# A transformer layer in split fp32: squares by tokens, roots and column sums off GpSimd, stored weight sums, and attention's transposes ahead of its scores

## The chip, the cores and the metric

One core of a Trainium2 chip runs the whole layer. The metric is the device time of one execution in microseconds, the median of three runs. Engines: TensorE (PE in the rows) multiplies, VectorE (DVE) and ScalarE (ACT) compute on tiles, GpSimd (POOL) does element-wise work and issues some DMAs, SyncE (SP) issues the other DMAs. SBUF is the on-chip memory, PSUM the memory that TensorE writes to, in banks of 128 x 512 fp32.

## The reference

A layer over 2048 tokens of width 1024, all in fp32: chunked attention with 16 heads of 64 and a learned relative bias, then a SwiGLU feed-forward part of width 2816.

```python
def rms_norm(x, g):
    y = xf * lax.rsqrt(jnp.mean(xf * xf, axis=-1, keepdims=True) + RMS_EPS)
    return (y * g.astype(jnp.float32)).astype(x.dtype)

h = rms_norm(x, g_pre_mix[i])
m = chunk_relpos_attention(h, w_qkv[i], w_o[i], rel_bias[i // N_MIXERS])
x = x + rms_norm(m, g_post_mix[i])
h = rms_norm(x, g_pre_ffn[i])
x = x + rms_norm(swiglu(h, w_gate[i], w_up[i], w_down[i]), g_post_ffn[i])
```

A chunk of 64 tokens attends to its own and the eight chunks before it, so a block of 128 queries sees 640 keys, five blocks of 128.

## The kernel before

**Products.** Each fp32 operand is split into a high and a low half (`split`, `split_part`; `hi` by ScalarE, `lo` by VectorE), and each product is three matmuls of 128x512 (`products`, L184 to L186). The large products run in seven instead of eight block products (Strassen's scheme): the blocks of activations and weights are B11, B21, T1, T2, B22, T4, T3, where T and S stand for sums of blocks. The weights' sums S1 to S4 are made by GpSimd in `block_items` (L816), in place in the raw tiles that were loaded; the splits then read them.

**Projection** (`project`). The 2048 tokens are two groups g of two 512-token blocks n. For each group `values_of` makes the values and `queries_keys` the queries and keys. The norm's gain goes into the activations; its root, one number per token, is applied behind the product: by `emit_v` for the values (tokens on partitions) and by `emit_qk` for q and k (tokens along the row, so a multiplication with `rows_of[n]`, the root spread over all partitions by four transposes, `spread`, tile prs, L336). The root of block n comes from squares of the activations on their way through `prep` (ScalarE's `sq`, L251), added up by GpSimd (`total`, L252), summed over partitions by TensorE (pssq, L269) and raised to -1/2 by GpSimd (L276). Group 1's activations are prepared while group 0's q and k are made. In `closing` VectorE takes a PSUM bank into `terms` (L1201), and `emit_qk` multiplies (L418), splits (L420, L421) and stores.

**Attention** (`Attend`). 32 jobs (four quarters n of 512 queries, eight pairs of heads p), four slots t each, one for each block of 128 queries. `scores` writes both heads' 640 scores to one tile `st` of three PSUM banks; VectorE adds the bias and finds the row's extreme (L506, `nmax`), ScalarE takes the exponentials (L510), VectorE the reciprocals (L514), GpSimd scales (L517). `transposed` transposes key blocks 0 to 3 of each head into `tt` (two banks, L532), copied out by VectorE for head 0 (L535) and by ScalarE for head 1 (L537), and then the fifth block of both heads into the free end of the scores' bank (L543, copied by ScalarE, L544). `output` multiplies with the values (L559). Between these stands filler, `fill`: the output projection of the quarter before, cut into small pieces. The first quarter has no filler, and, as nothing precedes it, no fifth block.

**Feed-forward** (`gate_up`, `down`, two token groups; stream `back` brings the weights of each of 11 column units, once for each group).

**Order.** TensorE's order is the order in which the code is written. The other engines' order comes from a list scheduler over the same program, so a change in the code can reorder them. Background steps (`later`, `timed`, `roots`) are released by the amount of TensorE work done. `Stream.ahead` loads and splits weights some blocks ahead of their use; SP issues nearly all DMAs in one queue in order. Raw weight tiles come from a ring of 8 (`w4`) in the projection, of 6 in the feed-forward part.

Of the kernel before, what the change touches and what calls it, by code (L numbers as in the profile page):

```python
# [9 lines left out]
F32 = mybir.dt.float32  # L10
# [3 lines left out]
ALU = mybir.AluOpType  # L14
# [35 lines left out]
def trunk(  # L50
    ctx: ExitStack,
    tc: tile.TileContext,
    x: bass.AP,
    gains: bass.AP,
# [359 lines left out]
    def emit_qk(n, p, which, src, eng=dve):  # L414

        scale = (0.125, 1.0)[which]
        t = narrow("t")
        eng.tensor_tensor(t, src, rows_of[n], op=ALU.mult)  # L418
# [10 lines left out]

    def scores_bank():  # L430

        if "S" not in phase:
            phase["S"] = phase["psa"].tile([P, 3 * HALF], F32, name="st", bufs=1)
        return phase["S"]

    class Attend:
# [45 lines left out]
        def scores(self, ib):  # L482
# [16 lines left out]
            rows = ap.tile([P, 4], F32, tag="rows", name="rows", bufs=3)  # L499
# [21 lines left out]
        def transposed(self, ib, fill):  # L521
# [16 lines left out]
            fill()  # L538
            if self.prev:
                r, b = blocks[4]  # L540
                tt = scores_bank()[:, 1280:1536].rearrange("p (h q) -> p h q", h=2)
                for h in range(2):
                    pe.transpose(tt[:, h, :], sc[h][:, b * P : b * P + P], ident)  # L543
                act.activation(self.pT[:, :, 4, cols], tt, AF.Copy)  # L544
# [42 lines left out]
    class Blocks:  # L587
# [58 lines left out]
        def build(self, part, w, prep):  # L646
# [32 lines left out]
            def t2(k):  # L679
# [5 lines left out]
                pool.tensor_tensor(b, b, c, op=ALU.subtract)  # L685
                pool.tensor_tensor(a, d, a, op=ALU.subtract)
# [118 lines left out]

    def block_items(src, key, early=True, ahead=None):

        r = {}

# [5 lines left out]
        def sum_(to, a, b, op=ALU.add):  # L815
            last_pool[0] = pool.tensor_tensor(r[to], r[a], r[b], op=op)  # L816

        def make(n):
# [3 lines left out]
            if n == ("B11" if early else "B21"):  # L822
                sum_("A21", "A21", "A22")
                sum_("A11", "A11", "A21")
            if n == "B21":
                sum_("A12", "A12", "A11")
            if n == "T2":
                sum_("A21", "A11", "A22", ALU.subtract)
# [10 lines left out]
    def v_items(g):  # L839

        parts = [block_items(w_v[h], f"v{g}{h}", False, {n: (8, 2 + h) for n in BLOCKS}) for h in range(2)]
# [288 lines left out]
    def values_of(g, b, big):  # L1130
# [9 lines left out]
        def after(name, m, pt):  # L1140
# [31 lines left out]
    def queries_keys(g, b, big, after):  # L1172
# [13 lines left out]
        for c in range(NPAIR // 2):  # L1186
# [12 lines left out]
            def closing(pts, terms, n, p, op=ALU.subtract):  # L1199
                def go(i):  # L1200
                    dve.tensor_tensor(terms[i], pts[i], terms[i], op=op)  # L1201
                    emit_qk(n, p, i, terms[i], pool)
# [26 lines left out]
    def project():  # L1229
# [10 lines left out]
        def prepare(g):  # L1240
            def prep(t, k, x_):
                if k == 0:
                    totals[2 * g + t] = (
                        io("total") if g else phase["fp"].tile([P, HALF], F32, tag="tot", name="total", bufs=2)
                    )
                add_square(x_, totals[2 * g + t], k == 0, pool)
# [16 lines left out]

        front.ahead(-8)
# [8 lines left out]
        for k, (_, f) in enumerate(build(0, "B11")):  # L1273
            f()
            if k == 0:
                front.ahead(-2)
        later.extend(timed(
            (1.0, build(0, "B21", 2.5)), (14.0, build(0, "T1", 3.5)[:1]), (17.0, roots(0, 2.0)),
            (20.0, build(0, "T1", 3.0)[1:]), (30.0, build(0, "T2", 4.0)), (47.0, roots(1, 4.0)),
            (53.0, build(0, "B22", 2.0)), (62.0, build(0, "T4", 2.0)), (71.0, build(0, "T3", 1.0)),  # L1280
            (100.0, [(0.0, bias_rows)]),
        ))
        for g in range(NG):
            big = xp.tile([P, 10, HALF], F32, tag="big", name="terms", bufs=1)
            yield from values_of(g, groups[g], big)
            drain()

            def after(name, g=g):
# [288 lines left out]
```

## Time and profile before

| | |
|---|---|
| three runs | 2672.91, 2688.82, 2688.07 us; median 2688.07 |
| profiled execution | 2675.12 us on the device, span 2673.4 us, mean TensorE clock 0.964 |
| busy | TensorE 90%, VectorE 65%, ScalarE 43%, GpSimd 30% of the span |
| DMA | 461.06 MB moved, 172 GB/s in the mean |
| stages | projection 0 to 592 us, attention 592 to 1305, feed-forward to the end |

Rows of groups give: line, engine, operation, output and inputs by the program's names, count, then busy us and mean ns of one, then the engine's idle us just before them and what ended it. Rows of waits give the waiting engine and line, what it waited for, us in total, times and the longest. Rows of a timeline give start, duration, engine and line, and in brackets the idle time before and its releaser.

### The profile page before, as it was taken

The page shows a single profiled execution, that of the slowest core. Times are in us where ns is not written, and L with a number is a line of the kernel's source. Part 1 is how long each engine was busy: PE and PEld are TensorE (multiplying, and loading weights), DVE is VectorE, ACT ScalarE, POOL GpSimd, SP SyncE. Part 2 cuts the span into 40 slices and gives each one's busy share as a digit, 9 for nine tenths or more (in the row PEclk, how much of TensorE's full clock was granted, in tenths as well). Part 3 has the DMA queues.
Part 4 walks back from the last instruction along what each step waited for, and adds up shares of the span by engine and source line. Part 5 has one row for each costly group of instructions (what it writes and reads, how often), then busy time and mean ns, then how long its engine had stood idle before and what let it go on. Part 6 is the DMA issues. An engine that isn't in the chain of part 4 may idle for free. (4 is left out here: it accounts for less than half of the span.)

```text
span 2673.4 us, 33185 instructions
## 1 busy us (share of the span) xinstructions
PE 2419.3 (90%) x11466; PEld 1938.0 (72%) x11466; DVE 1739.1 (65%) x2470; ACT 1153.4 (43%) x2039; POOL 809.5 (30%) x598
## 2 busy tenths in 40 slices
PE   7988779977888788887899999999999999999998
PEld 5776658765566566666687778888887788888887
DVE  7755866655544454555598768767756778765567
ACT  6522543325554444445453233336543233333444
POOL 7434755543322332232143222210003222220002
PEclk7999889988999999999999999999999999999999
DMA  4344439969865675667345544327764354427554
GB/s 158 121 123 128 154 103 281 284 170 229 227 174 163 181 209 159 190 203 199 126 142 189 177 146 131 107 74 260 254 213 154 131 175 148 151 84 246 186 185 162
DMA packets 210921, 461.06 MB, mean 172 GB/s; under 512 B 24224, under 2 KB 40624, under 8 KB 206272
## 3 DMA queue, kind: packets, MB, share of 16 engines
q1 hardware_dynamic: 208640, 447.39, 53.5%
q0 software_dynamic: 2112, 11.54, 2.5%
q8 instruction: 91, 1.49, 0.2%
q14 instruction: 78, 0.64, 0.1%
HBM read 347.11 MB, written 134.79 MB: 180 GB/s over the span
## 5 line engine op out<-in xcount | busy, mean ns | idle before, releaser
L816 POOL TENSOR_TENSOR raw<-raw,raw 128x1024 f32<-128x1024 f32 x136 | 358.9, 2640 | 911.2 <-DMA raw<-in_w_gu 439.6
L517 POOL TENSOR_SCALAR sc<-sc,rows 128x640 f32<-128x640 f32 (+4 forms) x256 | 191.5, 762 | 465.0 <-DVE rows L514 297.0
L510 ACT ACTIVATE sc<-sc,nmax 128x640 f32<-128x640 f32 (+4 forms) x256 | 192.9, 754 | 218.4 <-DVE nmax L506 215.0
L506 DVE CUSTOM_DVE_ANT_0 sc<-st,bias 128x640 f32<-128x640 f32 (+2 forms) x248 | 175.9, 746 | 154.1 <-PE st L498 130.7
L497 PE MATMUL st<-k,q 128*128 128x512 f32 (+3 forms) x440 | 153.9, 362 | 113.5 <-ACT pT L544 95.3
L184 PE MATMUL pb<-hb,w_wg_T 128*128 128x512 f32 x528 | 207.3, 393 | 8.0 <-DVE terms L918 7.3
L186 PE MATMUL pb<-hb,w_wg_T 128*128 128x512 f32 x528 | 206.9, 392 | 0.0
L185 PE MATMUL pb<-hb,w_wg_T 128*128 128x512 f32 x528 | 206.6, 391 | 0.0
L497 PEld LDWEIGHTS st<-k,q 128*128 128x128 f32 x440 | 86.7, 197 | 146.0 <-ACT pT L544 117.3
L185 PE MATMUL pd<-a,w_d_T 128*128 128x512 f32 (+1 forms) x368 | 140.5, 382 | 1.8 <-DVE a L341 1.8
L186 PE MATMUL pd<-a,w_d_T 128*128 128x512 f32 (+1 forms) x368 | 140.6, 382 | 0.1
L920 ACT ACTIVATE terms<-terms 128x512 f32<-128x512 f32 x65 | 41.1, 632 | 230.7 <-DVE terms L918 230.7
L184 PE MATMUL pd<-a,w_d_T 128*128 128x512 f32 (+1 forms) x368 | 140.6, 382 | 0.0
L184 PE MATMUL pa<-hb,w_wg_B 128*128 128x512 f32 x352 | 137.3, 390 | 1.8 <-ACT terms L899 1.8
L186 PE MATMUL pa<-hb,w_wg_B 128*128 128x512 f32 x352 | 137.0, 389 | 0.0
L185 PE MATMUL pa<-hb,w_wg_B 128*128 128x512 f32 x352 | 136.9, 389 | 0.0
L532 PEld LDWEIGHTS tt<-ident,sc 128*128 128x128 f32 x928 | 110.2, 145 | 30.6 <-POOL sc L517 15.4
L498 PE MATMUL st<-k,q 128*128 128x512 f32 (+3 forms) x440 | 132.3, 333 | 0.0
L131 DVE TENSOR_TENSOR w_wg_T<-raw,w_wg_T 128x1024 fp32r<-128x1024 f32 x88 | 123.6, 1405 | 11.6 <-ACT w_wg_T L130 11.5
L559 PE MATMUL po<-pT,v 128*64 128x128 f32 (+3 forms) x864 | 130.6, 451 | 0.0
L532 PE MATMUL tt<-ident,sc 128*128 128x128 f32 x928 | 129.5, 282 | 0.0
L421 DVE SCALAR_TENSOR_TENSOR lo<-t,hi 128x512 fp32r<-128x512 f32 x64 | 72.8, 1137 | 76.8 <-ACT hi L420 76.7
(253 smaller groups left out, 6515.1 us busy)
## 6 DMA issues: line engine op xcount, KB each, us to landing
raw<-in_w_gu SPq DMA_DIRECT2D x88, 512.0 KB, 4.0
q<-q SPq DMA_DIRECT2D x62, 512.0 KB, 6.6
k<-k SPq DMA_DIRECT2D x55, 512.0 KB, 8.4
raw_a<-aT SPq DMA_DIRECT2D x88, 256.0 KB, 3.8
raw_d<-d_S SPq DMA_DIRECT2D x88, 256.0 KB, 3.5
bias<-ext_d SPq DMA_DIRECT2D x124, 144.0 KB, 8.8
aT<-T SPq DMA_DIRECT2D x66, 256.0 KB, 2.0
raw_d<-in_w_d SPq DMA_DIRECT2D x66, 256.0 KB, 4.0
```

What stands on the lines that cost most here:

```text
L131: dve.tensor_tensor(lo, raw, hi.bitcast(F32), op=ALU.subtract)
L184: pe.matmul(pt, a_hi, b_hi, start=first, stop=False, skip_group_check=go_on)
L185: pe.matmul(pt, a_hi, b_lo, start=False, stop=False, skip_group_check=go_on)
L186: pe.matmul(pt, a_lo, b_hi, start=False, stop=last, skip_group_check=go_on)
L497: pe.matmul(st[:, a:b], q[:, 2 * h, cols], kk[:, h, key], start=True, stop=False)
L498: pe.matmul(st[:, a:b], q[:, 2 * h + 1, cols], kk[:, h, key], start=False, stop=True)
L506: dve.tensor_tensor_reduce(out=sc[:, :n], in0=st[:, c0 : c0 + n], in1=rev, scale=-1.0, scalar=3.0e38, op0=ALU.add, op1=ALU.min, accum_out= ...
L510: act.activation(sc[:, :n], sc[:, :n], AF.Exp, bias=nmax, scale=-1.0, accum_out=rows[:, h : h + 1])
L517: last_pool[0] = pool.tensor_scalar(sc[:, :n], sc[:, :n], rows[:, 2 + h : 3 + h], 1.0, op0=ALU.mult, op1=ALU.mult)
L532: pe.transpose(tt[:, u, :], sc[h][:, b * P : b * P + P], ident)
L559: pe.matmul(po[heads[h], c0:c1], v[:, kb, c : c + 64], self.pT[:, h, r, c0:c1], start=m == 0, stop=m == len(terms) - 1,)
L816: last_pool[0] = pool.tensor_tensor(r[to], r[a], r[b], op=op)
```

## The change

Four things change.

1. The roots of blocks 1 to 3 are made from a second copy of the input, `xt`, with tokens on partitions: ScalarE squares a 128x1024 tile with its row sum as a by-product (`roots_by_tokens`), and GpSimd raises four columns to -1/2. Block 1 uses one spare tile for its four loads. Block 0 keeps the old way, with the adds on VectorE.
2. VectorE does what GpSimd did at three places: the multiplication by the root in `closing`, in place, the two subtractions of `t2`, and the addition of values in `after`.
3. Group 0 stores every weight sum to DRAM (`sums_d`) by a DMA that GpSimd issues; group 1 loads the stored sums (`stored_items`) and makes none, for the projection and for gate and up.
4. In attention a slot is now: transposes of slot t, scores of slot t + 3, filler, fifth block of slot t. Before: scores of slot t + 2, filler, transposes of slot t, filler, fifth block. The fifth block goes to a `tt` bank.

```diff
-    def emit_qk(n, p, which, src, eng=dve):
+    def emit_qk(n, p, which, src, t=None):
-        t = narrow("t")
-        eng.tensor_tensor(t, src, rows_of[n], op=ALU.mult)
+        if t is None:
+            t = narrow("t")
+        dve.tensor_tensor(t, src, rows_of[n], op=ALU.mult)
...
-                cuts = [(0, 512, 640), (640, 1024, 1280)]
+                cuts = [(P, 512, 768), (768, 1024, 1408)]
...
-            st = scores_bank()
+            st = phase["psa"].tile([P, 3 * HALF], F32, tag="S", name="st", bufs=1)
...
-                sc = ap.tile([P, 640], F32, tag="sc", name="sc", bufs=6)
-                nmax = ap.tile([P, 1], F32, tag="nmax", name="nmax", bufs=6)
+                sc = ap.tile([P, 640], F32, tag="sc", name="sc", bufs=8)
+                nmax = rows[:, 4 + h : 5 + h]
...
-            fill()
-            if self.prev:
-                r, b = blocks[4]
-                tt = scores_bank()[:, 1280:1536].rearrange("p (h q) -> p h q", h=2)
-                for h in range(2):
-                    pe.transpose(tt[:, h, :], sc[h][:, b * P : b * P + P], ident)
-                act.activation(self.pT[:, :, 4, cols], tt, AF.Copy)
+            self.rest = (sc, blocks[4], cols) if self.prev else None
+
+        def fifth(self):
...
+            tt = phase["psa"].tile([P, 4, P], F32, tag="tt", name="tt", bufs=2)
+            for h in range(2):
+                pe.transpose(tt[:, h, :], sc[h][:, b * P : b * P + P], ident)
+            act.activation(self.pT[:, :, 4, cols], tt[:, 0:2, :], AF.Copy)
...
-                pool.tensor_tensor(b, b, c, op=ALU.subtract)
-                pool.tensor_tensor(a, d, a, op=ALU.subtract)
+                dve.tensor_tensor(b, b, c, op=ALU.subtract)
+                dve.tensor_tensor(a, d, a, op=ALU.subtract)
...
+    def stored_items(src, key, ahead=None):
+        def load(n):
+            a = FACTOR[n]
+            t = phase["fp"].tile([P, 1024], F32, tag="w4", name="raw4", bufs=phase["w4"])
+            sp.dma_start(t, src[BLOCK_AT[a]] if a in BLOCK_AT else sums_d[key][a])
+            return t
...
-        def sum_(to, a, b, op=ALU.add):
-            last_pool[0] = pool.tensor_tensor(r[to], r[a], r[b], op=op)
+        def sum_(name, to, a, b, op=ALU.add):
+            pool.tensor_tensor(r[to], r[a], r[b], op=op)
+            last_pool[0] = pool.dma_start(sums_d[key][name], r[to])
...
-                pool.tensor_tensor(z[m], z[m], p1[m], op=ALU.add)
+                dve.tensor_tensor(z[m], z[m], p1[m], op=ALU.add)
...
-                    emit_qk(n, p, i, terms[i], pool)
+                    emit_qk(n, p, i, terms[i], terms[i])
...
-                add_square(x_, totals[2 * g + t], k == 0, pool)
+                if g == t == 0:
+                    add_square(x_, totals[0], k == 0)
...
+        def roots_by_tokens(n, w, back, room=None):
...
+            def load(b):
...
+                c[b] = room or phase["fp"].tile([P, D], F32, tag="w4", name="xt", bufs=phase["w4"])
+                sp.dma_start(c[b], xt[4 * n + b])
+
+            def use(b):
+                act.activation(c[b], c[b], AF.Square, accum_out=c["sum"][:, b : b + 1])
+
+            def root():
+                m = const.tile([P, 4], F32, tag="ms", name="ms", bufs=2)
+                dve.tensor_scalar(m, c["sum"], 1.0 / D, EPS, op0=ALU.mult, op1=ALU.add)
+                pool.tensor_tensor(rs[n], m, neg_half.to_broadcast([P, 4]), op=ALU.pow)
...
-            (20.0, build(0, "T1", 3.0)[1:]), (30.0, build(0, "T2", 4.0)), (47.0, roots(1, 4.0)),
-            (53.0, build(0, "B22", 2.0)), (62.0, build(0, "T4", 2.0)), (71.0, build(0, "T3", 1.0)),
+            (20.0, build(0, "T1", 3.0)[1:]), (30.0, build(0, "T2", 3.5)), (45.0, roots_by_tokens(1, 0.5, 2.0, spare)),
+            (52.0, build(0, "B22", 2.0)), (62.0, build(0, "T4", 2.0)), (71.0, build(0, "T3", 1.0)),
...
+            if g == 0:
+                later.extend(pause(50.0) + roots_by_tokens(2, 8.0, 4.0) + pause(10.0) + roots_by_tokens(3, 8.0, 4.0))
...
-                        (12.0, roots(2, 3.0)), (15.0, roots(3, 3.0)),
...
-        job.scores((t + 2) % 4)
...
-        fill(0.45 * share)
         if t > 0 and t % 4 == 0:
+            fill(0.45 * share)
             jobs[t // 4 - 1].output()
...
-        if t >= 0:
-            jobs[t // 4].transposed(t % 4, lambda: fill(0.55 * share))
-        if t < 0:
-            fill(0.55 * share)
+        job = jobs[t // 4]
+        job.transposed(t % 4)
+        ahead(t + AHEAD)
+        fill((0.55 if t % 4 == 0 else 1.0) * share)
+        job.fifth()
```

Three places show how instructions move. VectorE's order where group 0's q and k are closed, before (`terms` are the sums of q or k, `lo` the low half, `raw` and `w` a weight on its way to being split):

```order
84 L1201 TENSOR_TENSOR terms<-pb,terms 128x512
85 L421 SCALAR_TENSOR_TENSOR lo<-t,hi 128x512
86 L1201 TENSOR_TENSOR terms<-pb,terms 128x512
87 L131 TENSOR_TENSOR w_w_T_1178<-raw_1015,w_w_T_1178 128x1024
88 L421 SCALAR_TENSOR_TENSOR lo<-t,hi 128x512
```

The same place after the change:

```order
110 L1224 TENSOR_TENSOR terms<-pb,terms 128x512
111 L420 TENSOR_TENSOR terms<-terms,row 128x512
112 L423 SCALAR_TENSOR_TENSOR lo<-terms,hi 128x512
113 L1224 TENSOR_TENSOR terms<-pb,terms 128x512
114 L132 TENSOR_TENSOR w_wq_T_1239<-raw_1077,w_wq_T_1239 128x1024
115 L420 TENSOR_TENSOR terms<-terms,row 128x512
```

The multiplication by the root (L420) now stands on VectorE between the sum and the low half. GpSimd's order at the same stage, before (L816 are weight sums, L418 the multiplication):

```order
36 L816 TENSOR_TENSOR raw_671<-raw_661,raw_673 128x1024
37 L816 TENSOR_TENSOR raw_1308<-raw_1308,raw_1310 128x1024
38 L816 TENSOR_TENSOR raw_966<-raw_966,raw_1015 128x1024
39 L418 TENSOR_TENSOR t<-terms,total 128x512 x2
40 L816 TENSOR_TENSOR raw_968<-raw_968,raw_966 128x1024
41 L418 TENSOR_TENSOR t<-terms,total 128x512 x2
```

And after:

```order
31 L834 TENSOR_TENSOR raw_719<-raw_719,raw_729 128x1024
32 L835 DMA s_q_S_193<-raw_719 128x1024
33 L834 TENSOR_TENSOR raw_721<-raw_721,raw_719 128x1024
34 L835 DMA s_q_S_195<-raw_721 128x1024
35 L834 TENSOR_TENSOR raw_729<-raw_719,raw_731 128x1024
36 L835 DMA s_q_S_194<-raw_729 128x1024
```

The multiplications are gone from between the sums, and each sum is followed by a store of it to DRAM. ScalarE's order in the middle of attention, before (L510 exponentials, L537 copy of head 1's four transposes, L544 copy of the fifth block):

```order
557 L510 ACTIVATE sc,rows<-sc,nmax 128x640 x2
558 L537 ACTIVATE pT<-tt 128x4x128
559 L544 ACTIVATE pT<-st 128x2x128
560 L510 ACTIVATE sc,rows<-sc,nmax 128x640 x2
561 L537 ACTIVATE pT<-tt 128x4x128
```

And after (L506 exponentials, L533 copy of head 1, L543 copy of the fifth block):

```order
556 L506 ACTIVATE sc,rows<-sc,rows 128x640 x2
557 L533 ACTIVATE pT<-tt 128x4x128
558 L506 ACTIVATE sc,rows<-sc,rows 128x640 x2
559 L543 ACTIVATE pT<-tt 128x2x128
560 L533 ACTIVATE pT<-tt 128x4x128
```

The copy of a slot's fifth block now follows the exponentials of later scores and reads a `tt` bank.

More of the change, by code (lines that the diff above doesn't have):

```diff
@@ L53, in trunk @@
     x: bass.AP,
+    xt: bass.AP,
     gains: bass.AP,
@@ L1461, in trunk, with ahead @@
     per = slots // NQ
-    for t in range(-2, slots):
-        if t + 2 < slots:
-            job = jobs[(t + 2) // 4]
-            job.scores((t + 2) % 4)
-            if (t + 2) % 4 == 1 and (t + 2) // 4 + 1 < len(jobs):
-                jobs[(t + 2) // 4 + 1].load()
+    AHEAD = 3
+    def ahead(t):
+        if t < slots:
+            jobs[t // 4].scores(t % 4)
+            if t % 4 == 1 and t // 4 + 1 < len(jobs):
+                jobs[t // 4 + 1].load()
+    for t in range(AHEAD):
+        ahead(t)
+    for t in range(slots):
         share = (0.4 if t % 4 == 0 else 1.2) * left[0] / max(per - t % per - 1, 1)
-        fill(0.45 * share)
         if t > 0 and t % 4 == 0:
+            fill(0.45 * share)
             jobs[t // 4 - 1].output()
```

63 lines of the change are left out of this document (44 added, 19 removed).

## Prediction

> **What bounds the kernel now.** I read the table of busy time by stage first, then TensorE's waits, then the timeline at the places that the waits name. The stages are: projection 0 to 592 us, attention 592 to 1305 (its first quarter, without filler, up to 700), the feed-forward part after it.
>
> ```profile
> core 0: us, PE busy (x) PEld busy (x) DVE busy (x) ACT busy (x) POOL busy (x), PEclk, DMA share, GB/s
> 0.00:100.00 100.00, 77.85 (x293) 59.85 (x294) 78.59 (x65) 60.36 (x96) 73.22 (x43) 0.85 0.35 128
> 100.00:300.00 200.00, 176.36 (x734) 143.02 (x732) 115.24 (x124) 75.08 (x108) 80.36 (x41) 0.95 0.49 154
> 300.00:360.00 60.00, 30.29 (x107) 23.58 (x108) 54.05 (x36) 26.32 (x43) 56.77 (x30) 0.69 0.19 53
> 360.00:592.00 232.00, 219.36 (x952) 179.01 (x950) 140.19 (x148) 83.08 (x114) 113.35 (x91) 0.98 0.81 230
> 592.00:700.00 108.00, 81.16 (x453) 60.55 (x452) 61.26 (x220) 62.42 (x184) 41.34 (x80) 0.86 0.96 232
> ...
> 905.00:1112.00 207.00, 170.84 (x1036) 126.94 (x1032) 104.55 (x224) 101.80 (x225) 64.09 (x73) 0.98 0.65 184
> ...
> 1990.00:2673.00 683.00, 665.20 (x2973) 551.22 (x2971) 468.55 (x589) 259.13 (x393) 130.31 (x54) 0.99 0.50 165
> ```
>
> TensorE is the engine that all others feed. In the feed-forward stage it is busy for 97% of the time, so only its own work counts there. In the projection and the attention it is not: 300 to 360 is half empty with VectorE and GpSimd both over 90% busy, and an attention quarter leaves 36 us of 207 unused. The first quarter is short of DMA (0.96 busy). What ends TensorE's waits in the whole run:
>
> ```profile
> PE st L497 <- ACT pT L544: 95.3, 93, 3.3
> PE pb L184 <- DVE terms L1201: 31.2, 9, 11.5
> PE st L497 <- DVE nmax L506: 20.7, 17, 6.0
> PE prs L336 <- POOL hr L276: 18.2, 2, 14.4
> PE pa L184 <- ACT terms L1193: 17.1, 6, 5.9
> ...
> PE pb L184 <- DVE terms L918: 7.3, 3, 3.9
> ...
> PE pssq L269 <- POOL total L252: 4.8, 1, 4.8
> ...
> PE st L497 <- DMA k<-k: 4.4, 2, 2.5
> ```
>
> The columns are us in total, times, longest. The first row is attention: scores wait for ScalarE's copy of the fifth key block, which sat in the scores' own bank. Rows two, four, five and seven belong to the projection, and two of their waits lie in the half-empty stretch of 60 us:
>
> ```profile
> PE prs L336 <- POOL hr L276: 14.4, 1, 14.4
> PE pb L184 <- DVE terms L1201: 13.3, 2, 11.5
> ```
>
> Why VectorE is late there is seen in the timeline:
>
> ```profile
> 301.58 1.73 POOL L252 TENSOR_TENSOR total<-total,sq 128x512 f32<-128x512 f32 x1
> 302.09 1.77 DVE L341 TENSOR_TENSOR hb<-hb,hb 128x512 fp32r<-128x512 f32 x1
> 303.28 2.81 POOL L816 TENSOR_TENSOR raw<-raw,raw 128x1024 f32<-128x1024 f32 x1
> 303.79 2.85 DVE L421 SCALAR_TENSOR_TENSOR lo<-t,hi 128x512 fp32r<-128x512 f32 x1
> ...
> 315.43 3.41 POOL L252 TENSOR_TENSOR total<-total,sq 128x512 f32<-128x512 f32 x2
> 315.94 0.68 DVE L1201 TENSOR_TENSOR terms<-pb,terms 128x512 f32<-128x512 f32 x1
> ...
> 316.67 0.80 PE L184 MATMUL pb<-hb,w_w_T 128*128 128x512 f32 x1 [11.50 <-DVE terms L1201]
> ```
>
> Each VectorE operation with both inputs in SBUF ends 0.55 us after the GpSimd operation that had begun before it (301.58 + 1.73 + 0.55 = 302.09 + 1.77), while the one whose input is PSUM takes its 0.68 beside GpSimd. So GpSimd's work is paid twice: on GpSimd and as VectorE's waiting. L1201 itself is short; it stands behind such operations in VectorE's queue and TensorE waits 11.5 us for its bank.
>
> **Projection.** The prices:
>
> ```profile
> L816 POOL TENSOR_TENSOR raw<-raw,raw 128x1024 f32<-128x1024 f32 x136 | 358.9, 2640 | 911.2 <-DMA raw<-in_w_gu 439.6 <-issue 136.1 <-DVE w_wg_B L131 97.7
> L418 POOL TENSOR_TENSOR t<-terms,total 128x512 f32<-128x512 f32 x48 | 78.0, 1634 | 62.5 <-DVE terms L1201 53.2 <-DMA k<-hi 6.8 <-issue 2.1
> L774 POOL DMA_DIRECT2D d_S<-in_w_d x22 | 21.1, 1048 | 11.5 <-DMA d_S<-in_w_d 11.5
> ...
> L130 ACT ACTIVATE w_wv_T<-raw 128x1024 fp32r<-128x1024 f32 x16 | 16.7, 1052 | 10.3 <-issue 8.0 <-PE pv L186 2.3
> ```
>
> ```profile
> raw<-in_w_v SPq DMA_DIRECT2D x16, 512.0 KB, 7.6
> ...
> d_S<-d_S POOLq DMA_DIRECT2D x22, 256.0 KB, 6.5
> ```
>
> - The 48 multiplications by the root (L418) leave GpSimd: 1.63 us there, an estimated 0.68 on VectorE (the duration of L1201, same shape). They stand between L1201 and the pair hi/lo, and VectorE's `lo` waits behind them, so each of the 48 chains is a microsecond shorter, and more where a 2.64 us sum stood ahead of it in GpSimd's queue. VectorE gets 48 x 0.68 = 33 us more to do and the subtractions besides, over stages in which it is busy for 255 us of 432 (100 to 300 and 360 to 592). Of the 31.2 + 17.1 = 48 us in rows two and five I count three quarters, **-36**. The last quarter stays because group 0 keeps its 24 sums on GpSimd, beside which a moved operation, with both its inputs in SBUF, takes 1.75 to 2.85 us as in the rows above.
> - The Trainium skill, page "SBUF — State Buffer", section "Who interferes with whom", says that a VectorE instruction with two SBUF inputs contends with a GpSimd instruction that reads SBUF, and that the loser fully blocks. The rows agree (302.09 against 315.94). The rule speaks against this part of the change in group 0: were the moved operations there held for whole sums, the 24 us in which TensorE is idle between 100 and 300 would stay, and with them some 16 of my 36: 2571 in place of the sum below.
> - The roots of blocks 1 to 3 come from tokens: 12 loads of 512 KB (7.6 us to landing) and 12 squares of 128x1024 on ScalarE (1.05 us, as a copy of that size) in place of 24 squares and GpSimd's adds. The wait of 14.4 us at 354 is for the root of a group-1 block that was summed amid the crowd at 300 to 350; it is now made tens of microseconds ahead, **-14**. Next in line there are the weights of the values, whose group-1 sums are gone too. Block 0's adds go to VectorE, **-5** (row seven).
> - The stretch 300 to 360 runs at clock 0.69: 0.283 us of busy time for each of its 107 matmuls against 0.230 from 360 on. Without the long waits it should run like the rest, 107 x 0.053 = **-5**.
> - Block 1's four loads share one buffer (`spare`), so they form a chain of 4 x (7.6 + 1.05) = 35 us with SP's later loads queued behind each. It starts at about 45 and its root is needed for the values of block 1. I take **+5** for it; bounds 0, if it is ready in time, and +20, a chain that starts 20 us late.
>
> Together -55. Bounds: if every moved operation is held by GpSimd's sums in group 0 and only the stretch 300 to 360 is cured, -20; if all listed waits go, about -85.
>
> In VectorE's order after the change the multiplication stands between L1224 (L1201 before) and `lo`; the next L1224, which frees TensorE's bank, waits for these two and for ScalarE's `hi`, but no more for GpSimd.
>
> **Stored sums.** Group 0 makes its 68 sums as before and issues 68 stores (1.05 us of GpSimd each, 71 us); group 1 drops 68 sums (180 us) and loads 17 x 3 blocks of 512 KB more. In the feed-forward part of group 1 DMA is 0.50 busy, so the loads hide; what goes is part of the few waits like L918's, **-3** (0 to -8). In 360 to 592 it is 0.81 busy: the 6 units of v, q and k add 18 loads, 9.4 MB, or 33 us at 230 / 0.81 = 284 GB/s, against 0.19 x 232 = 44 us of idle DMA. It just fits; I take **+3** from later k loads (row eight) and keep 0 and +33.
>
> **Attention.** One plain slot:
>
> ```profile
> 1017.80 0.50 PE L497 MATMUL st<-k,q 128*128 128x512 f32 x1 [0.80 <-ACT pT L544]
> ...
> 1019.51 0.82 DVE L506 CUSTOM_DVE_ANT_0 sc<-st,bias 128x640 f32<-128x640 f32 x1 [1.84 <-PE st L498]
> ...
> 1020.26 0.82 DVE L506 CUSTOM_DVE_ANT_0 sc<-st,bias 128x640 f32<-128x640 f32 x1
> ...
> 1021.01 0.69 DVE L535 COPY pT<-tt 128x512 f32<-128x512 f32 x1
> ...
> 1021.27 0.82 ACT L510 ACTIVATE sc<-sc,nmax 128x640 f32<-128x640 f32 x1
> ...
> 1022.08 0.57 ACT L537 ACTIVATE pT<-tt 128x512 f32<-128x512 f32 x1
> 1022.14 0.38 PE L543 MATMUL st<-ident,sc 128*128 128x128 f32 x2
> ...
> 1022.56 0.38 ACT L544 ACTIVATE pT<-st 128x256 f32<-128x256 f32 x1
> ...
> 1022.99 0.50 PE L497 MATMUL st<-k,q 128*128 128x512 f32 x1 [0.47 <-ACT pT L544]
> ```
>
> From scores to scores 5.19 us: scores, two reductions (to +3.28), exponentials (to +4.29), the copies L537 and L544, next scores.
>
> In ScalarE's order after the change the fifth block's copy (L543) stands behind the exponentials of the next scores (L506), and its bank is no longer the scores'. Scores then wait for their bank only until the reductions end, +3.28, but behind transposes that need one of two `tt` banks. Three cases: (a) the bank is free, as after an output: about +3.4; (b) it was emptied by VectorE's copy behind the reductions: 3.28 + 0.69 + four transposes, an estimated 0.6 (two take 0.38 in L543) = +4.6; (c) it held the fifth block, whose copy stands behind the exponentials: 4.29 + 0.38 + 0.6 = +5.3, no better than now. A job has four slots; with one (a), one (b), one (c) and 0.3 us in the slot of the output it saves 1.8 + 0.6 + 0 + 0.3 = 2.7 us, and three quarters hold 24 jobs: **-65** of the 95 us of row one. Bounds: 0 by (c) alone, and -95, when all of row one goes. The first quarter has no fifth block and stays as it is.
>
> **Sum.** -55 - 3 + 3 - 65 = -120. The profiled execution took 2675.1 us on the device (span 2673.4), so 2555. The median of the three runs, 2688, is 13 above it; I predict against the profiled one.
>
> **Rivals.**
> 1. *The attention wait changes hands*: case (c) in nearly every slot, TensorE waits at the transposes for ScalarE. For it: the copy stands behind the exponentials in the new order. Against: banks alternate and VectorE's copies free half of them. 2675 - 55 = 2620. Chance 0.2.
> 2. *Both stages clear fully*: -85 in the projection, -95 in attention, -8: 2487. For it: TensorE has idle room for it (36 us in one quarter). 0.15.
> 3. *The projection keeps its lock*: group 0's sums hold the moved operations and block 1's chain stalls, so -20 in place of -55: 2590. 0.1.
> 4. *Slower: stores hold the weight ring.* A raw buffer is free only when its store has landed (6.5 us after an issue of 1.05), and the load that waits for it blocks all loads behind it in SP's queue. Exposed in each of the 17 units of group 0, it eats the gain from 120 / 17 = 7 us a unit on, one landing; with 10 us it gives 2555 + 170 = 2725. Against: GpSimd is idle for 911 us ahead of L816 and loads run units ahead. 0.06.
>
> The Trainium skill, page "SBUF — State Buffer", section "A bandwidth-pool intuition that's wrong", would add to rival 4: a DMA issued from GpSimd that takes about 0.62 us takes 3.1 beside a VectorE copy that locks the port. By that page the 68 stores would cost GpSimd up to an estimated 211 us, not 71. The mean of 1.05 for L774's issues, beside a VectorE that was 60% busy, speaks against so much.
>
> **How the numbers follow.** The forecast holds 0.49, own range 2510 to 2595. For 8 in 10 I reach to most of rival 2 and rival 1 with a part of the DMA bound above it: 2485 to 2640. About 1% is what a measurement of this kernel can tell from no change. Faster by more than that: all but rival 4 and the worst of rival 1 with DMA on top, 0.89; same 0.05; slower 0.06.
>
> **What would show it.** Right: GpSimd near idle from 300 on, VectorE's `lo` near 1.1 us there, no TensorE wait above 5 us at 300 to 360, the wait of st on the fifth copy gone and what is left of it named tt; a quarter of attention some 22 us shorter. Wrong: tt waiting on ScalarE for 80 us or more (rival 1), prs or values waiting near 60 to 90 (block 1's chain), SP's loads waiting on GpSimd stores (rival 4), first-quarter scores waiting on k.

## The result, and the profile after

The changed kernel took 2505.22 us (median of four runs, 2502.53 to 2506.91) against 2680.49 for the kernel before in the same runs: a ratio of 0.9347, 95% interval 0.9304 to 0.9389. The profiled execution took 2506.2 us (span 2504.4), 168.9 less than the profiled one of before; the forecast was 120 less, 2555, with a range from 2485 to 2640. The result lies inside that range, a little below the narrower one of 2510 to 2595.

Where it went is read from three moments: the first scores matmul, the last product with the values, and the end. The rows of these lines (minimum, median and maximum in ns, then first and last start in us), of before and then of after:

```profile
L497 PE MATMUL st<-hb x8: 274/552/796, 592.6 to 605.1; 128*128 128x128 f32 x2, 128*128 128x256 f32 x2, 128*128 128x384 f32 x2, 128*128 128x512 f32 x2
...
L559 PE MATMUL po<-pT,v x864: 272/454/1117, 639.4 to 1317.1; 128*64 128x128 f32 x45, 128*64 128x256 f32 x44, 128*64 128x512 f32 x42, 128*64 128x384 f32 x42
```

```profile
L493 PE MATMUL st<-hb x8: 220/552/796, 518.1 to 529.8; 128*128 128x128 f32 x2, 128*128 128x256 f32 x2, 128*128 128x384 f32 x2, 128*128 128x512 f32 x2
...
L558 PE MATMUL po<-pT,v x864: 272/432/644, 563.0 to 1162.8; 128*64 128x128 f32 x46, 128*64 128x384 f32 x43, 128*64 128x256 f32 x43, 128*64 128x512 f32 x41
```

So the projection went from 592.6 to 518.1 (-74.5), attention from 724.5 to 644.7 (-79.8), the rest from 1356.3 to 1341.6 (-14.7). How much of this is waiting is seen in the pages' rows of busy time, before and then after:

```profile
PE 2419.3 (90%) x11466; PEld 1938.0 (72%) x11466; DVE 1739.1 (65%) x2470; ACT 1153.4 (43%) x2039; POOL 809.5 (30%) x598
```

```profile
PE 2360.5 (94%) x11442; PEld 1914.6 (76%) x11442; DVE 1672.8 (67%) x2557; ACT 1162.8 (46%) x2039; POOL 498.2 (20%) x490
```

TensorE's idle time, the span less its busy time, fell from 254.1 to 143.9 us, by 110; its busy time fell too, by 59, with nearly as many matmuls. The stages of after:

```profile
core 0: us, PE busy (x) PEld busy (x) DVE busy (x) ACT busy (x) POOL busy (x), PEclk, DMA share, GB/s
0.00:100.00 100.00, 77.01 (x288) 59.74 (x289) 80.05 (x88) 62.01 (x97) 31.27 (x26) 0.85 0.53 200
100.00:300.00 200.00, 186.95 (x810) 152.98 (x809) 150.21 (x178) 95.53 (x142) 49.41 (x32) 0.98 0.68 229
300.00:360.00 60.00, 60.00 (x266) 49.69 (x266) 40.84 (x54) 31.69 (x46) 6.91 (x9) 1.00 0.77 227
360.00:518.00 158.00, 158.00 (x699) 130.87 (x698) 97.11 (x128) 55.79 (x75) 29.06 (x48) 1.00 0.98 298
518.00:610.00 92.00, 67.65 (x392) 50.19 (x391) 54.95 (x201) 54.69 (x166) 32.08 (x62) 0.91 0.97 251
610.00:1163.00 553.00, 492.75 (x3132) 380.27 (x3131) 322.91 (x683) 321.92 (x696) 186.83 (x213) 0.99 0.74 204
```

From 300 us to the end of the projection TensorE is busy all the time, at full clock; the half-empty stretch is gone. The last column but one warns: DMA is now 0.98 busy there. TensorE's waits after:

```profile
PE st L493 <- DVE rows L502: 29.9, 34, 5.2
PE tt L528 <- DVE pT L531: 21.5, 23, 1.1
PE tt L528 <- ACT pT L543: 13.8, 20, 1.3
PE pb L185 <- DVE terms L1224: 13.1, 5, 4.0
PE prs L337 <- POOL hr L1302: 9.6, 1, 9.6
PE mm L185 <- ACT w L131: 6.9, 2, 3.7
PE tt L528 <- DVE rows L510: 6.3, 6, 1.1
```

The 95 us for the fifth block's copy are gone from st; 41.6 stand at the transposes (rows two, three and seven). The 48 us on terms are 13.1, all between 100 and 300, where group 0's sums still run. What the lock of GpSimd and VectorE is worth is seen in one operation at the two places. The multiplication L420 in group 0 and in group 1 (count, then busy us and mean ns):

```profile
L420 DVE TENSOR_TENSOR terms<-terms,row 128x512 f32<-128x512 f32 x16 | 20.6, 1290 | 0.3
```

```profile
L420 DVE TENSOR_TENSOR terms<-terms,row 128x512 f32<-128x512 f32 x23 | 15.9, 689 | 0.4
```

The mean of 1290 ns hides two kinds, as the timeline of after shows:

```profile
198.51 2.40 POOL L834 TENSOR_TENSOR raw<-raw,raw 128x1024 f32<-128x1024 f32 x1
...
198.70 2.77 DVE L420 TENSOR_TENSOR terms<-terms,row 128x512 f32<-128x512 f32 x1
```

Of the 24 multiplications in place in group 0 (these 16 and 8 with the row of block 0), 7 began while a sum was running and ended about 0.55 us after it; they took 1.90 to 2.77 us. The other 17, two of them begun just ahead of a sum, took 0.68 to 0.69, as without sums.

### The profile page after: what moved, and what is told of

Read it like the earlier page. It is cut to its first block, busy times and chain, and to the rows that moved or that the text cites. A ratio compares the mean times of both kernels' runs of the same rounds, so it can differ in the third digit from the quotient of the medians.

```text
span 2504.4 us, 33018 instructions
## 1 busy us (share of the span) xinstructions
PE 2360.5 (94%) x11442; PEld 1914.6 (76%) x11442; DVE 1672.8 (67%) x2557; ACT 1162.8 (46%) x2039; POOL 498.2 (20%) x490
## 3 DMA queue, kind: packets, MB, share of 16 engines
q8 instruction: 91, 1.49, 0.3%
## 4 chain that ended last, share of the span: by engine, by line
PE 54%; DVE 2%; ACT 1%; issue 1%; DMA 0%; POOL 0%; DVEq 0%; SPq 0%; ACTq 0%
PE pd L187 6%; PE pd L185 6%; PE pd L186 6%; PE pb L186 4%; PE pb L187 4%; PE pb L185 4%; PE pc L186 3%; PE pc L187 3%; PE pc L185 3%; PE pa L185 3%; PE pa L186 3%; PE pa L187 3%; PE po L558 1%; PE mm L187 1%; PE mm L185 1%; PE mm L186 1%
## 5 line engine op out<-in xcount | busy, mean ns | idle before, releaser
L834 POOL TENSOR_TENSOR raw<-raw,raw 128x1024 f32<-128x1024 f32 x68 | 179.9, 2646 | 394.3 <-DMA raw<-in_w_gu 139.6
L506 ACT ACTIVATE sc<-sc,rows 128x640 f32<-128x640 f32 (+4 forms) x256 | 192.9, 755 | 112.6 <-DVE rows L502 112.4
L528 PE MATMUL tt<-ident,sc 128*128 128x128 f32 x928 | 140.6, 281 | 45.6 <-DVE pT L531 21.5
L277 POOL TENSOR_TENSOR rs<-ms,neg_half 128x4 f32<-128x4 f32 (+1 forms) x7 | 7.9, 1125 | 854.8 <-DVE ms L275 854.8
L528 PEld LDWEIGHTS tt<-ident,sc 128*128 128x128 f32 x928 | 105.0, 143 | 82.2 <-issue 72.1
L493 PE MATMUL st<-k,q 128*128 128x384 f32 (+3 forms) x440 | 140.7, 340 | 28.0 <-DVE rows L502 23.1
L494 PE MATMUL st<-k,q 128*128 128x384 f32 (+3 forms) x440 | 129.9, 315 | 0.0
L531 DVE COPY pT<-tt 128x512 f32<-128x512 f32 (+3 forms) x128 | 81.6, 637 | 69.6 <-ACT hb L341 36.2
L342 DVE TENSOR_TENSOR a<-raw_a,a 128x512 fp32r<-128x512 f32 x154 | 105.7, 694 | 30.1 <-ACT a L341 29.9
L558 PE MATMUL po<-pT,v 128*64 128x384 f32 (+3 forms) x864 | 125.2, 436 | 0.0
```

Of the source, the lines that this page charges most:

```text
L342: eng.tensor_tensor(lo, src, hi.bitcast(F32), op=ALU.subtract)
L493: pe.matmul(st[:, a:b], q[:, 2 * h, cols], kk[:, h, key], start=True, stop=False)
L494: pe.matmul(st[:, a:b], q[:, 2 * h + 1, cols], kk[:, h, key], start=False, stop=True)
L506: act.activation(sc[:, :n], sc[:, :n], AF.Exp, bias=nmax, scale=-1.0, accum_out=rows[:, h : h + 1])
L528: pe.transpose(tt[:, u, :], sc[h][:, b * P : b * P + P], ident)
L558: pe.matmul(po[heads[h], c0:c1], v[:, kb, c : c + 64], self.pT[:, h, r, c0:c1], start=m == 0, stop=m == len(terms) - 1,)
```

## The experiments

Each run changes the kernel before or after as its short diff says. The stages were read from each run's trace in the same way as above; they belong to one profiled execution, so they need not add up to the median:

| kernel | us, median | ratio to before, interval | to first scores | attention | rest |
|---|---|---|---|---|---|
| before | 2680 | | 592.6 | 724.5 | 1356 |
| after | 2505.2 | 0.9347 (0.9304 to 0.9389) | 518.1 | 644.7 | 1342 |
| undo_attention | 2587.5 | 0.9650 (0.9624 to 0.9677) | 517.0 | 720.6 | 1341 |
| undo_moves | 2543.4 | 0.9489 (0.9468 to 0.9509) | 547.6 | 644.5 | 1348 |
| undo_stored | 2524.3 | 0.9418 (0.9391 to 0.9444) | 535.2 | 638.4 | 1349 |
| undo_roots | 2519.1 | 0.9405 (0.9379 to 0.9432) | 532.7 | 639.3 | 1344 |
| attention_alone | 2593.3 | 0.9670 (0.9636 to 0.9704) | 594.3 | 640.6 | 1357 |
| moves_alone | 2635.3 | 0.9832 (0.9804 to 0.9860) | 550.8 | 728.1 | 1357 |
| stored_alone | 2654.9 | 0.9914 (0.9889 to 0.9939) | 568.9 | 736.1 | 1347 |
| own_bank_old_order | 2495.5 | 0.9306 (0.9273 to 0.9339) | 519.8 | 634.5 | 1343 |
| fifth_in_scores | 2542.8 | 0.9483 (0.9447 to 0.9518) | 522.7 | 678.3 | 1340 |
| fifth_first | 2489.7 | 0.9281 (0.9243 to 0.9320) | 518.7 | 627.5 | 1342 |
| fifth_leads | 2514.4 | 0.9384 (0.9360 to 0.9409) | 518.3 | 647.8 | 1342 |
| leads_early_root | 2520.0 | 0.9404 (0.9382 to 0.9427) | 524.1 | 651.4 | 1343 |

**One part undone.** First the attention of before:

```diff
+            st = scores_bank()
...
+                tt = scores_bank()[:, 1280:1536].rearrange("p (h q) -> p h q", h=2)
...
+            job.scores((t + 2) % 4)
...
+        fill(0.45 * share)
...
-        job.transposed(t % 4)
-        ahead(t + AHEAD)
-        fill((0.55 if t % 4 == 0 else 1.0) * share)
-        job.fifth()
+        if t >= 0:
+            jobs[t // 4].transposed(t % 4, lambda: fill(0.55 * share))
```

> The changed kernel with the attention of before (scores, filler, transposes, filler, fifth block in the scores' bank); the other three parts stay. Theory: attention gained 80 us (from first scores to last output 724.5 to 644.7 us) by itself, through the chain over the fifth block's copy, so this takes 2505 + 80 = 2585, with the wait of st on the copy of pT back at about 95 us. Rival: attention gained because VectorE, GpSimd and the DMA queues are less crowded, and the new order only renames the wait; then this stays below 2540.

It took 2587.5, 82 more; the profiled executions differ by 75, all in attention (720.6 against 644.7), and the old wait is back as it was:

```profile
PE st L499 <- ACT pT L546: 94.5, 93, 3.3
```

Fewer GpSimd operations elsewhere do not help attention: the rival falls.

```diff
-        dve.tensor_tensor(t, src, rows_of[n], op=ALU.mult)
+        t = narrow("t")
+        eng.tensor_tensor(t, src, rows_of[n], op=ALU.mult)
...
-                dve.tensor_tensor(b, b, c, op=ALU.subtract)
-                dve.tensor_tensor(a, d, a, op=ALU.subtract)
+                pool.tensor_tensor(b, b, c, op=ALU.subtract)
+                pool.tensor_tensor(a, d, a, op=ALU.subtract)
...
-                dve.tensor_tensor(z[m], z[m], p1[m], op=ALU.add)
+                pool.tensor_tensor(z[m], z[m], p1[m], op=ALU.add)
...
-                    emit_qk(n, p, i, terms[i], terms[i])
+                    emit_qk(n, p, i, terms[i], pool)
```

> The changed kernel with the multiplication by the root, the two subtractions of T2 and the addition of values on GpSimd again. Theory: these operations behind GpSimd's 2.64 us sums were what made terms late, so most of the projection's gain goes: of the 74 us that it gained, about 36 come back, 2541. Rival: the stored sums alone free GpSimd in group 1, and the moved operations cost only in group 0: about 15 us, 2520.

2543.4, 38 more: 29.5 in the projection, 7 in the feed-forward part, whose blocks T2 are subtracted there too. The wait for terms is 21.7 us again:

```profile
PE pb L185 <- DVE terms L1223: 21.7, 6, 5.9
...
PE prs L337 <- POOL hr L1301: 12.3, 1, 12.3
```

```diff
-            last_pool[0] = pool.dma_start(sums_d[key][name], r[to])
...
+            last_pool[0] = pool.tensor_tensor(r[to], r[a], r[b], op=op)
...
-            items.extend(stored_items(w_qk[c], f"q{c}", ahead) if g else block_items(w_qk[c], f"q{c}", True, ahead))
+            items.extend(block_items(w_qk[c], f"{g}{c}", True, {"B11": (6, 2), "T1": (6, 2)} if c == 0 else None))
```

> The changed kernel with the weight sums made by GpSimd in both groups and none stored or loaded. Theory: group 1 of the projection runs without waits from 300 us on because of the missing sums; with them VectorE is held again as in group 0, where TensorE still waits 3 to 4 us once per pair, so 10 to 20 us there, and the feed-forward part gives back the 10 us that it gained: 2530. Rival: the moved operations alone are enough, and the stores and loads were of no use: 2505 or a little less, since 69 MB of traffic go.

2524.3, 19 more: 17 in the projection, 7 in the feed-forward part, and 6 less in attention. The sums for group 1 do hold VectorE. The longest wait of terms is 11.5 us, as long as in the kernel before; it ends at 286.6 us, still in group 0's products, behind three sums in a row (270.6 to 279.6) that GpSimd makes ahead for group 1. From 360 us on terms are waited for 7.3 us, in after not at all.

```profile
PE pb L185 <- DVE terms L1200: 26.4, 10, 11.5
...
PE prs L337 <- POOL hr L1278: 13.3, 1, 13.3
```

That attention is 6 us shorter without the stored sums may be their price: its first quarter takes 87.2 us from its first scores to the next quarter's, 91.3 in after, and the loads of stored sums fill the DMA engines just ahead of it (0.98 in the row above). It is not shown, for the first quarter takes 91.8 in attention_alone and 93.3 in the kernel before, neither of which has stored sums.

```diff
-                if g == t == 0:
-                    add_square(x_, totals[0], k == 0)
...
+                add_square(x_, totals[2 * g + t], k == 0, pool)
...
-            (20.0, build(0, "T1", 3.0)[1:]), (30.0, build(0, "T2", 3.5)), (45.0, roots_by_tokens(1, 0.5, 2.0, spare)),
...
+            (20.0, build(0, "T1", 3.0)[1:]), (30.0, build(0, "T2", 4.0)), (47.0, roots(1, 4.0)),
...
+                        (12.0, roots(2, 3.0)), (15.0, roots(3, 3.0)),
```

> The changed kernel with the roots of all blocks from squares of the activations again (added up on VectorE, as block 0 before was on GpSimd). Theory: the wait of 9.6 us for block 1's row at 76 goes or shrinks, and block 2's or 3's root comes a little late again, but without the 14 us wait, since GpSimd is free: 2505 to 2515. Rival: the roots by tokens carry the gain at 300 to 360, and this takes 2525 or more.

The expectation names VectorE for the adds; in the kernel that ran they are on GpSimd, as in the kernel before. It took 2519.1, between the two claims: the projection is 14.6 us longer, attention 5 shorter (why stays open). Block 1's wait of 9.6 is gone; the 3.6 us at prs stand at 313 us, before the first row of group 1, where the kernel before waited 14.4, as the theory said. Between 300 and 360 TensorE is idle for 7 us, where the changed kernel has none, so the rival holds in a small part. Block 0's total waits for GpSimd again:

```profile
PE pv L184 <- ACT hb L340: 10.4, 6, 4.1
PE pssq L269 <- POOL total L252: 4.7, 1, 4.7
...
PE prs L336 <- POOL hr L276: 3.6, 1, 3.6
```

The four undone parts cost 82 + 38 + 19 + 14 = 153 of the 175 us. The other 22 belong to no part alone. They do not lie in the projection only: by the stages of the table, moves, stored sums and roots give 61 of the projection's 74.5 back, and in attention, where undoing stored sums and roots makes it shorter, the four give 64 of 79.8.

**One part alone.** Attention first, the kernel before with the new `Attend` and slot loop (the first diff, the other way round).

> The kernel before with the new attention alone. Theory: attention and projection are separate, so it gains its 80 us: 2680 - 80 = 2600. Rival: it needs GpSimd free of sums or of the d_S traffic, and gains less than 60.

2593.3, 89 less than the 2682.5 of before in those runs: attention is a problem of its own. Moves alone (the second diff, the other way round, on the kernel before):

> The kernel before with the moved operations alone (multiplication by the root, subtractions of T2, addition of values on VectorE). Theory: the three parts of the projection share one cause, the crowd on GpSimd, so a part alone takes most of what is to be had: undoing the moves cost 38 us, moves alone gain 50 or more, 2630 or less. Rival: the parts add up and the moves alone gain 38 or less, 2642 or more.

45 less than 2680.1, between the claims, a little more than undoing them cost.

> The kernel before with the stored weight sums alone. Theory of the shared crowd: more than the 19 us that undoing them cost, 25 to 50, 2630 to 2655, since group 1's chains of GpSimd multiplications no longer stand behind sums. Rival: 19 or less, 2661 or more. If stores hold the weight ring in group 0, TensorE's waits between 100 and 300 grow over the 22 us of before.

25 less, at the near edge of the shared crowd. The stores did not hold the weight ring: between 100 and 300 TensorE waits 17.9 us, 22.4 before. But the first quarter of attention grew from 93.3 to 101.3, and k is waited for:

```profile
PE st L497 <- DVE nmax L506: 24.1, 16, 8.7
...
PE st L497 <- DMA k<-k: 8.9, 3, 5.6
```

**What in the attention did it.** The old order, that is undo_attention, with one edit, the fifth block's bank (its copy then reads `tt[:, 0:2, :]`):

```diff
-                tt = scores_bank()[:, 1280:1536].rearrange("p (h q) -> p h q", h=2)
+                tt = phase["psa"].tile([P, 4, P], F32, tag="tt", name="tt", bufs=2)
```

> The attention of before (its order, two slots ahead) with one edit: the fifth block goes to a tt bank and not to the free end of the scores' bank; the other three parts of the change stay. Theory that the bank was the cost: scores wait only for the reductions of the scores before, ScalarE has the fifth copy ahead of the next exponentials, and nearly all of the 82 us by which the run without the new attention was slower come back: 2505 to 2525. Rival, that the order is needed: with one more user of the two tt banks the transposes wait instead, 2560 or more.

2495.5: 92 us less than undo_attention (86 less in the attention of the profiled executions), and 10 less than the changed kernel. The fifth block's place was the cost; swapping the order gained nothing beside it. That it lost 10 us is at the edge of what the runs tell apart: the two intervals in the table overlap, though attention is 10.2 shorter in the profiled executions too. TensorE's waits:

```profile
PE st L499 <- DVE nmax L508: 23.7, 21, 5.3
PE tt L545 <- DVE pT L537: 18.9, 26, 3.0
...
PE tt L545 <- ACT pT L539: 9.3, 8, 2.3
```

Here the fifth copy stands ahead of the next exponentials, so hardly any transposes wait for it (0.8 us, once). The opposite edit, the new order with the fifth block in the scores' tile:

```diff
-            tt = phase["psa"].tile([P, 4, P], F32, tag="tt", name="tt", bufs=2)
+            st = last_st[0]
...
-                pe.transpose(tt[:, h, :], sc[h][:, b * P : b * P + P], ident)
+                end = st[:, 1408 * h : 1408 * h + P]
+                pe.transpose(end, sc[h][:, b * P : b * P + P], ident)
```

> The changed kernel in its new order, but with the fifth block's two transposes in the free first and last 128 columns of the scores' tile. Theory that the bank was the cost: the next scores wait for the copy of the fifth block behind the exponentials again, 4.3 + 0.4 us after the scores at the earliest, so most of the 82 us return: 2560 to 2590. Rival, that the order is what counts: 2505 to 2530.

2542.8: 38 more, between the two claims. With a shared bank the new order is 45 us better than the old one (2587.5), since the fifth block now waits mostly for the reductions and not for the exponentials:

```profile
PE st L546 <- DVE rows L505: 63.9, 64, 3.4
PE st L496 <- DVE rows L505: 21.7, 20, 5.3
...
PE st L496 <- ACT pT L548: 6.0, 9, 1.2
```

So each edit alone helps, the bank by 92 us and the order by 45, and both together are no better than the bank alone, by the medians 10 us worse.

Was it the bank or the tile? The first piece of a slot's scores, in the kernel before:

```profile
L497 PE MATMUL st<-k,q 128*128 128x512 f32 x110 | 54.8, 498 | 98.3 <-ACT pT L544 95.3 <-DVE nmax L506 2.9
```

All 95.3 us stand ahead of this piece, which writes columns 0 to 511, the first of the tile's three banks. The fifth block lay in columns 1280 to 1535, in the third. So in these rows the scores wait for the copy before they write to its bank: what tied them together was the common tile, and moving the fifth block changed tile and bank at once. A place in another bank of the same tile was not tried by itself.

**Beyond the change.** The fifth block third in the slot, ahead of the next scores:

```diff
+        part = 0.55 if t % 4 == 0 else 1.0
         job.transposed(t % 4)
+        fill(0.3 * part * share)
+        job.fifth()
         ahead(t + AHEAD)
-        fill((0.55 if t % 4 == 0 else 1.0) * share)
-        job.fifth()
+        fill(0.7 * part * share)
```

> The changed kernel with the slot as transposes, 0.3 of the filler, fifth block, next scores, 0.7 of the filler, so that ScalarE copies the fifth block ahead of the next exponentials. Theory: the plain slots of 4.7 to 5.6 us are set by the copies behind reductions and exponentials (tt on pT of VectorE 21.5 us, of ScalarE 13.8 us); without them they fall to TensorE's own work, 25 to 45 us faster than the changed kernel: 2460 to 2480. Rival: scores then wait for the reductions of the scores before (29.9 us now) or ScalarE and VectorE are the bound, so no more than 10 us: 2495 to 2505.

2489.7, the fastest of all, 15.5 less than the changed kernel, between the two claims: the wait went from the transposes to the fifth block itself, which needs the bank that VectorE empties.

```profile
PE tt L542 <- DVE pT L531: 31.2, 50, 1.9
...
PE tt L542 <- ACT pT L533: 5.4, 10, 0.8
```

To take that away, the fifth block first in the slot:

```diff
+            self.fifth()
             for h in range(2):
                 part = blocks[:4]
...
-        job.fifth()
```

> The changed kernel with the fifth block ahead of the four others: fifth, head 0, head 1, next scores, filler. Theory: head 1's transposes then wait only for ScalarE's short copy (0.38 us) made while head 0 is transposed, and the wait for VectorE's copy of head 0 that was left with the fifth block in third place (31.2 us in 50 waits) goes: 10 to 25 us less than that run, 2465 to 2480. Rival: the wait turns into one for the scores' reductions or ScalarE is behind with exponentials, 2485 to 2500.

2514.4, slower than both claims, and 9 more than the changed kernel. The four transposes now wait, for VectorE's copy and 46 times for the fifth's own:

```profile
PE tt L530 <- DVE pT L533: 26.6, 30, 1.0
PE tt L530 <- ACT pT L544: 18.3, 46, 1.6
```

Block 1's root earlier, on top of that:

```diff
-            (20.0, build(0, "T1", 3.0)[1:]), (30.0, build(0, "T2", 3.5)), (45.0, roots_by_tokens(1, 0.5, 2.0, spare)),
+            (20.0, build(0, "T1", 3.0)[1:]), (29.0, roots_by_tokens(1, 0.5, 2.0, spare)), (34.0, build(0, "T2", 3.0)),
```

> As fifth_leads, and block 1's loads and squares begin 16 us of TensorE work earlier, ahead of block 0's T2. Theory: the 9.6 us for which TensorE waits for block 1's row at 76 is the end of a chain of four loads and squares through one buffer, and goes: 8 to 10 us less than fifth_leads. Rival: the loads queue up ahead of T2's in SP's queue and T2 is late instead: no gain.

2520.0, 6 more than fifth_leads, so the theory falls. The row's four transposes come a fixed amount of TensorE work after the squares, so they moved forward with them, and the chain through the one buffer did not get shorter (from the first square to the last 17.4 us in after, 19.0 here); of after and then of this run:

```profile
76.63 1.11 PE L337 MATMUL prs<-ident,hr 128*128 128x128 f32 x4 [9.63 <-POOL hr L1302]
```

```profile
69.63 1.11 PE L337 MATMUL prs<-ident,hr 128*128 128x128 f32 x4 [14.86 <-POOL hr L1303]
```

TensorE came to the row at 54.8 us instead of 67.0, 12 us earlier, and the root only 7 us earlier.

## Why the prediction was right, and where not

- **What bounds it** held: waits of TensorE in projection and attention, from GpSimd's queue, the held VectorE, and the fifth block. Undoing each of the four parts gave time back.
- **The sum.** Waits were forecast at -115 us in all and TensorE's own work at -5 (the clock). Measured are -110 of idle time and -59 of busy time. So the waits came out nearly as added up, and the step that failed is the term for TensorE's work, counted for the 60 us at 300 alone. That 169 lies inside the wide range is in part luck: attention's waits fell less than forecast, and its busy time, which I had at nothing, made up for it.
- **Projection, forecast -55, measured -74.5.** The waits went about as counted: terms from 48.3 to 13.1 (-35, forecast -36), block 2's 14.4 gone (-14), pssq from 4.8 to 0.9 (-4, forecast -5), block 1's row from 3.9 to 9.6 (+6, forecast +5; the sign "prs waiting near 60 to 90" came, at this price). By the rows of the stages, idle time went from 88.1 to 36.0, -52 against -50 forecast, and busy time from 503.9 to 482.0, -22 against -5. Of the 22, the 24 short matmuls that the roots no longer need (eight take 1.49 us in after) are an estimated 4.5 at most. The rest goes with the clock: its mean by the same rows was 0.92 before and is 0.96 after, and 504 us of work at that ratio is an estimated 21 us. I had counted one row of the four, and 100 to 300 (0.95) and 360 to 592 (0.98) gained as well.
- **The lock in group 0** held as weighed: L420 takes 1290 ns there in the mean and 689 without sums, and the only waits left for terms are there. VectorE's `lo`, which I had expected near 1.1 us from 300 on, takes 0.69. By the Trainium skill's page "SBUF — State Buffer", section "Who interferes with whom", a VectorE instruction with two SBUF inputs contends with a GpSimd instruction that reads SBUF; the seven held multiplications agree. The 2571 that I worked out for a group 0 without gain did not come, since only those seven of 24 were held and 100 to 300 fell from 24 us idle to 13.
- **Stored sums, forecast -3 and +3, measured -15 in the feed-forward part.** undo_stored and undo_moves each give 7 of it back; the subtractions of T2, which also run there, I had not counted in that stage. The DMA cost that I expected at k did not show in after, where k is waited for 4.4 us as before; with the stored sums alone it was 8.9, and attention 12 us longer.
- **Rival 4**, stores that hold the weight ring, did not come. The stores were cheaper than my rows:

```profile
L835 POOL DMA_DIRECT2D s_g_S<-raw x44 | 25.5, 580 | 17.7 <-POOL raw L834 16.9 <-DMA res<-in_x 0.4 <-DMA y<-o 0.4
```

  0.58 us an issue instead of 1.05, and 3.1 to landing instead of 6.5. The Trainium skill's page "SBUF — State Buffer", section "A bandwidth-pool intuition that's wrong", gives 3.1 us for a DMA issued from GpSimd beside a VectorE copy. No run here tries that case: the longest of the 68 issues took 0.76 us, and what VectorE ran beside them in after were no copies.
- **Attention, forecast -65, measured -80; but the cause only half right.** The slots, seen from one to the next scores:

```profile
806.81 0.42 PE L493 MATMUL st<-k,q 128*128 128x384 f32 x1
...
810.02 0.45 PE L493 MATMUL st<-k,q 128*128 128x384 f32 x1 [0.37 <-DVE rows L502]
...
815.61 0.42 PE L493 MATMUL st<-k,q 128*128 128x384 f32 x1
...
820.57 0.66 PE L528 MATMUL tt<-ident,sc 128*128 128x128 f32 x4 [0.37 <-ACT pT L543]
820.98 0.42 PE L493 MATMUL st<-k,q 128*128 128x384 f32 x1
```

  3.21, 5.59 and 5.37 us: (a) at the reductions' floor, as forecast 3.4, and two longer ones, the second with a wait for the fifth copy as in (c). The mean of the second and third quarter went from 206.4 to 179.8, 3.3 us for each of eight jobs against 2.7 in the sum. But not by the waits that I counted. The three later quarters, before and then after:

```profile
686.00:1317.00 631.00, 521.71 (x3133) 388.51 (x3134) 320.68 (x684) 317.57 (x697) 184.22 (x213) 0.97 0.63 178
```

```profile
609.00:1163.00 554.00, 493.37 (x3134) 380.90 (x3134) 323.57 (x686) 322.92 (x698) 186.83 (x213) 0.99 0.74 204
```

  Idle time fell from 109 to 61, by 49 and not by 65, since 41.6 us of waits came up at the transposes; busy time fell by 28 for the same number of matmuls. The clock, 0.97 to 0.99, is an estimated 10 of these; the rest was not taken apart. What I took as one mechanism are two: the fifth block's place alone is worth 92 us, and the new order beside it gains nothing. The 13.8 us of waits for the fifth copy, case (c) and rival 1's mechanism, are not among the waits of the old order with its own bank.
- **Rivals 1 to 3**: 1 in part (41.6 us at the transposes, of them 13.8 for ScalarE's fifth copy), 3 not. The 2506 us lie nearer to rival 2's 2487 than to my 2555, but its condition, that all listed waits go, did not hold: 13.1 us for terms, 9.6 for block 1's row and those at the transposes stayed. What the parts share was not tried further: no run has the roots alone, or two parts.

## What to carry to other kernels

Work that two engines cannot do at the same time is paid on both; count a GpSimd sum's price also in the operations of VectorE that it holds. When long waits go, TensorE's own work can get shorter too: forecast its idle and its busy time apart, in every stage whose clock is below 1.00. A small block in the free end of a busy PSUM tile can tie that tile to its own reader: give it a tile of its own before changing the order, and try the one edit alone, as here it gave all that both gave. A background step that is released by work done can move its wait along with it.

## What the runs showed of the hardware

A DMA issue on GpSimd took 0.58 us for the store of a whole 512 KB tile (L835). The 256 KB DMAs of L774, which add from DRAM to DRAM, took 1.05 and 0.96 in the mean before, and 0.80 and 0.78 after (L773), on a GpSimd with less to do. A VectorE multiplication with both inputs in SBUF that began during a GpSimd sum ended about 0.55 us after it, and took 0.69 when it began ahead of one. The scores and the fifth block in the free end of their tile (columns 0 to 1279 and 1280 to 1535) did not overlap, yet scores waited for the copy, and already with the piece that lies in another bank; whether the chip or the program's own bookkeeping of tiles asks for it was not tried.
